# Start addresses of split weights and split activations in on-chip memory, by unused pads and two wider tiles

## The chip, the cores and the metric

One core of one Trainium2 chip runs the whole program. The metric is device microseconds of one execution of the program, as the median of several runs.

## What is computed

Two blocks on 256 tokens of width 1024, batch 1, all in float32. The first block is two layers; the second takes its output as x and is one layer with a small context of 256 tokens and a mixture of 16 experts. Cut to what matters here:

```python
def hybrid_layer(x, mem, pos, g_mix, w_in, w_pa, w_pb, w_pm, w_o, g_mem, w_mkv, g_mlp, w_up, w_down):
    h = rms_norm(x, g_mix)
    z = h @ w_in
    ...
    y = (gates[:, :, 0] * (o_a @ w_pa) + gates[:, :, 1] * (o_b @ w_pb)
         + gates[:, :, 2] * (o_m @ w_pm))
    x = x + y @ w_o
    hm = rms_norm(x, g_mlp)
    x = x + jnp.square(jax.nn.relu(hm @ w_up)) @ w_down
    return x
...
    x = x + g1[:, None, :] * out_l
    h_l = modulate(rmsnorm(x, norm2[l]), sh2, sc2)
    x = x + g2[:, None, :] * ec_moe(h_l, w_router[l], w_e_gate[l], w_e_up[l], w_e_down[l])
```

Behind `out_l` stand a latent attention with 8 heads and a gated recurrent mixer with 4 heads, both fed by projections with `w_in_2`. `ec_moe` lets each expert take 32 tokens and runs gate, up and down products of 1024 by 1024 for each.

## The kernel before, in words

**Split products.** All projections and the two MLPs are computed with split operands. A weight tile of 128 partitions by 2048 floats is loaded into pool `wrp` (tile `wr`, four buffers, `load_w`). `pieces` (L331) cuts it into pieces of 512 columns. ScalarE casts a piece to the format fp32r (the high part, L347), and VectorE, or at times GpSimd, subtracts the high part from the original and writes the rest (the low part, L353 and L351). Activations are split likewise into a high and a low part (`split_x`). `three` (L356) then issues three matmuls for a product: high weights with high activations, high with low, low with high. In `w_stationary` (L366) a block of 128 columns of the weights is loaded into TensorE and 256 columns of activations are streamed; in `x_stationary` (L378) it is the other way round. Every matmul has a weight load of its own, which TensorE issues while the matmul ahead of it runs. All matmuls of the helper `mm` carry line L290.

**Places.** The split pieces live in seven places, used in turn (L321 to L340): four in the tile `wh` of pool `whl`, three in a tile also named `wh` of pool `b1p`. `places.append(places.pop(0))` moves to the next place with every piece:

```python
    whx = whl.tile([128, 2, WH * PIECE], FR, tag="w", name="wh")
    wx_ = b1p.tile([128, 2, WX * PIECE], FR, name="wh")
```

When the second MLP is done, pool `b1p` is closed and the four places of `whl` remain (L1583). A place's high part and low part start at multiples of 2048 bytes from the start of their tile, and a block of 128 columns at multiples of 512, so the start of the tile modulo 128 bytes is the start of every operand in it modulo 128. The same holds for the split activations: `hx` (layer input, and the MLP's), `ux` (MLP hidden), `zq` (attention output), `mx` (memory), `xh` (context), `kvx` and `qx` (latents of the second block).

**Where tiles lie.** Pools are stacked from the low addresses in the order in which they are opened: `cst`, `per`, `sm`, `wrp`, `whl`, and behind them the pools of each stage (`lp0`, `ap0`, `mp0`, `bp`, `x2p` and so on). `b1p`, `ew0`, `yp`, `ew1` and `rt` are stacked from the high end downwards. A tile's size is rounded up to 32 bytes. So a pad moves all tiles stacked behind it.

**Order.** The program is in stages: memory keys; layer 0 (projections, three kinds of attention, gates, output product); its MLP; layer 1; its MLP; then the second block (context path, recurrent mixer, latent attention), up to about 1127 us; the router; and the experts. The order of TensorE is written by hand. In attention-like stages a `Filler` issues a few microseconds of projection matmuls between the links of a softmax chain. Weight loads are issued on SP's queue when a buffer comes free. The experts' weights (tile `ew`) are loaded into 23 slots made of freed tiles and then reused, on the same queue.

`readout` (L1350) scales the recurrent mixer's output; its tile `skip` is a column of 8 floats for each partition. `scg`, also 8 floats, is used once ahead of the second block (L1619). `srow` and `macc` (L567) are the last tiles of `b1p`.

Of the kernel before, what the change touches and what calls it, by code (L numbers as in the profile page):

```python
# [8 lines left out]
FT = mybir.dt.float32  # L9
# [214 lines left out]
def in_turn(*gens):  # L224

    gens = list(gens)
    while gens:
        g = gens.pop(0)
        for c in g:
            yield c  # L230
            if c is None:
                gens.append(g)
                break
# [8 lines left out]
def fused_kernel(ctx: ExitStack, tc: tile.TileContext, I, out):  # L242
# [5 lines left out]
    cst = ctx.enter_context(tc.tile_pool(name="cst", bufs=1))  # L248
    per = ctx.enter_context(tc.tile_pool(name="per", bufs=1))
    sm = ctx.enter_context(tc.tile_pool(name="sm", bufs=4))  # L250
    wrp = ctx.enter_context(tc.tile_pool(name="wrp", bufs=WR, reuse_waits="tile"))
    whl = ctx.enter_context(tc.tile_pool(name="whl", bufs=1, reuse_waits="tile"))
    accp = ctx.enter_context(tc.tile_pool(name="accp", bufs=2, space=PSUM))
    flp = ctx.enter_context(tc.tile_pool(name="flp", bufs=2, space=PSUM))
    wk = ctx.enter_context(tc.tile_pool(name="wk", bufs=2, space=PSUM))
# [17 lines left out]
    b1p = b1.enter_context(tc.tile_pool(name="b1p", bufs=1, side="right"))  # L273
# [8 lines left out]
    def vc(n, j=0, w=1):  # L282
        o = vcols[n][0] + j
        return vbuf[:, o:o + w]
# [4 lines left out]
    def mm(o, l, r, st, sp):  # L289
        PE.matmul(o, l, r, start=st, stop=sp, skip_group_check=True)  # L290
# [6 lines left out]
    def acc_tile(nm):  # L297
        return accp.tile([128, 512], FT, tag="acc", name=nm)

    def fl_tile(nm):  # L300
        return flp.tile([128, 512], FT, tag="fl", name=nm)
# [152 lines left out]
    def rstd_cols(ssum, n, nm, bank=None):  # L454

        ps = (bank or acc_tile)("ps_" + nm)
        halves = [ssum] if len(ssum.shape) == 2 else [ssum[:, i] for i in range(ssum.shape[1])]
        for t in range(2):
            for i, v in enumerate(halves):
                mm(ps[:, t:t + 1], v[:, t * 128:(t + 1) * 128], ones[:, 0:1], t + i == 0, i == len(halves) - 1)  # L460
        r = sm.tile([128, 2], FT, tag="rc_" + nm, name="rc_" + nm, bufs=2)
        with tc.high_priority(offset=HR):
            V.tensor_scalar(r, ps[:, 0:2], 1.0 / n, EPS, op0=OP.mult, op1=OP.add)
            G.tensor_tensor(r, r, mhalf[:, 0:2], op=OP.pow)
        return r

    def bcast_rows(col2, dst, bank=None):

        ps = (bank or acc_tile)("ps_bc")
        for t in range(2):  # L470
            across(ps[:, t * 128:(t + 1) * 128], col2[:, t:t + 1], t == 0)
        with tc.high_priority(offset=HB):
            V.tensor_copy(dst, ps[:, 0:256])

    def updated(dn):

        for j in range(4):
            if dn:
                V.tensor_tensor(xT[:, 2 * j:2 * j + 2], xT[:, 2 * j:2 * j + 2], pair(dn[j]), op=OP.add)
            yield 2 * j  # L480
            yield 2 * j + 1
# [84 lines left out]

    srow = [b1p.tile([128, 1024], FT, name="srow")]  # L567
    macc = b1p.tile([128, 2, 48], FT, name="macc")

    def layer(l, lp, ap, start):  # L570
        xs, ssum = start
# [379 lines left out]
    def pool(st, nm, side="left"):  # L951
        return st.enter_context(tc.tile_pool(name=nm, bufs=1, side=side, reuse_waits="tile"))
# [12 lines left out]
    def modulated(src, rb, sc, sh, tp, emit, eng=None):  # L965

        for k in range(8):
            t = tp.tile([128, 256], FT, tag="modt", name="modt", bufs=2)
            (eng or V).scalar_tensor_tensor(t, src[:, k], sc[:, k:k + 1], rb, op0=OP.mult, op1=OP.mult)
            emit(k, t, sh[:, k:k + 1])  # L970
            yield
# [377 lines left out]

    def readout(hm, ss, xc, tzg, tp):  # L1350

        skip = tp.tile([128, 8], FT, name="skip")
        V.tensor_scalar(skip, vc("mls", 0, 8), 0.5, None, op0=OP.mult)
        V.tensor_scalar(ss, ss, 1.0 / 256, EPS, op0=OP.mult, op1=OP.add)
        G.tensor_tensor(ss, ss, mhalf, op=OP.pow)
        for h in range(4):
            for t in range(2):
                hv = hm[:, t, h * 256:(h + 1) * 256]
                V.tensor_scalar(hv, hv, ss[:, t * 4 + h:t * 4 + h + 1], None, op0=OP.mult)
        F.fill(FRO[0])  # L1360
        for j in range(4):
            F.fill(FRO[1])
            ps = acc_tile("hT")
            for i in range(2):
                for t in range(2):
                    k = 2 * j + i
                    PE.transpose(ps[:, i * 256 + t * 128:i * 256 + t * 128 + 128], hm[:, t, k * 128:(k + 1) * 128],
                                 ident)
            u = tp.tile([128, 2, 256], FT, tag="ro", name="ro", bufs=2)
            for i in range(2):  # L1370
                k = 2 * j + i
                A.activation(u[:, i], xc[:, k], AF.Copy, scale=skip[:, k:k + 1])
                V.scalar_tensor_tensor(u[:, i], ps[:, i * 256:(i + 1) * 256], vc("mln", k), u[:, i], op0=OP.mult,
                                       op1=OP.add)
            sl = slice(2 * j, 2 * j + 2)
            V.scalar_tensor_tensor(u, tzg[0][:, sl], 1.0, u, op0=OP.add, op1=OP.mult)
            V.scalar_tensor_tensor(hm[:, :, j * 256:(j + 1) * 256], tzg[1][:, sl], 1.0, u, op0=OP.add, op1=OP.mult)
# [220 lines left out]
    with ExitStack() as es:  # L1598
        fp = pool(es, "b2c")
        xcc = fp.tile([128, 8, 256], FT, name="xcc")  # L1600

        def ctx_path():
            yield from in_turn(ml_features(cx, xcc, kTc, vex[0], gp, wg, fp),
                               keys_values(0, cx, kn[0], vt[0], kp0, fp))

        share[0] = SH1[0]
        cg = F.add(ctx_path())

        s1 = fp.tile([128, 256], FT, name="s1")
        s2 = fp.tile([128, 256], FT, name="s2")  # L1610
        for k in updated(dn):
            for s_, sc, eng in ((s1, 1.0, G), (s2, vc("g_fin", k), V)):
                d = s_ if k == 0 else fp.tile([128, 256], FT, tag="sqf", name="sq", bufs=3)
                A.activation(d, xT[:, k], AF.Square, scale=sc)
                if k:
                    eng.tensor_tensor(s_, s_, d, op=OP.add)
            F.fill(FX[2])
        share[0] = SH1[1]
        scg = fp.tile([128, 8], FT, name="scg")  # L1619
        V.tensor_tensor(scg, sc1[:, 0], vc("g_fin", 0, 8), op=OP.mult)  # L1620
        F.fill(FX[0])
        r1 = rstd_cols(s1, 1024, "fin")
        ps = acc_tile("ps_s2")
        for t in range(2):
            mm(ps[:, t:t + 1], s2[:, t * 128:(t + 1) * 128], ones[:, 0:1], t == 0, True)
        r2 = fp.tile([128, 2], FT, name="r2")
        V.scalar_tensor_tensor(r2, ps[:, 0:2], 1.0 / 1024, r1, op0=OP.mult, op1=OP.mult)
        V.tensor_tensor(r2, r2, r1, op=OP.mult)
        V.tensor_scalar(r2, r2, EPS, None, op0=OP.add)
        G.tensor_tensor(r2, r2, mhalf[:, 0:2], op=OP.pow)  # L1630
        V.tensor_tensor(r2, r2, r1, op=OP.mult)
        F.fill(FX[1])
        rb2 = fp.tile([128, 256], FT, name="rb2")
        bcast_rows(r2, rb2)
        rb1 = fp.tile([128, 256], FT, name="rb1")
        bcast_rows(r1, rb1)
        for _ in modulated(xT, rb2, scg, modT[:, 0, 0:8], fp, into(hh, hl)):
            F.fill(FX[3])
        share[0] = SH1[2]
        F.need(cg)  # L1640

        sh2 = modT[:, 0, 24:32]
        ss = per.tile([128, 8], FT, name="ssh")
        lb0 = per.tile([128, 16], FT, name="lb0")
        lb_ps = fl_tile("lb0")
        sw = fp.tile([128, 8, 16], FT, name="sw")
        V.tensor_tensor(sw, vc("wrt", 0, 128).rearrange("p (k e) -> p k e", k=8),
                        sh2[:, :, None].to_broadcast([128, 8, 16]), op=OP.mult)
        sws = fp.tile([128, 16], FT, name="sws")
        V.tensor_reduce(sws, sw.rearrange("p k e -> p e k"), axis=AX.X, op=OP.add)  # L1650
        mm(lb_ps[:, 0:16], ones, sws, True, True)
        V.tensor_copy(lb0, lb_ps[:, 0:16])
        for k in range(8):
            A.activation(xT[:, k], xT[:, k], AF.Copy, scale=vc("g_fin", k))
            G.tensor_tensor(xT[:, k], xT[:, k], rb1, op=OP.mult)
# [48 lines left out]
    with ExitStack() as es:  # L1704
        tp = pool(es, "b2k")
# [324 lines left out]
```

## Time and profile before

| what | value |
|---|---|
| median of three runs | 1569.76 us (1569.51 to 1571.85) |
| the profiled execution | 1572.26 us |
| its span in the trace | 1570.5 us |
| granted TensorE clock, mean over the span | 0.945 |
| TensorE matmuls, weight loads | 1372.3 us (87%), 1138.6 us (72%) |
| VectorE, ScalarE, GpSimd | 914.0, 666.6, 242.3 us |
| transfers | 404.87 MB, mean 258 GB/s |

Times of single instructions come from the profiled execution. PE is TensorE's matmul stream, PEld its weight loads, DVE is VectorE, ACT ScalarE, POOL GpSimd, SP the queue that issues the transfers. A matmul lasts longer than the distance to the next one, since they are pipelined; the distance (the step) is what counts in a dense stream, and a window cut at the start of a run and at the start of the next gives it. A clock of 1.00 is the full granted clock.

### The profile page before, as it was taken

The numbers are of one execution on the slowest core, as the hardware profiler recorded it, in microseconds if no ns is written. First come the engines' busy times: TensorE is split into PE (matmuls) and PEld (weight loads), VectorE is DVE, ScalarE is ACT, GpSimd is POOL, SyncE is SP. The second block draws the span as 40 slices with busy tenths as digits, with TensorE's granted clock in tenths as the row PEclk, the third lists the DMA queues.
The fourth block names the chain that finished last, engine by engine and source line by source line (L and its number), as shares of the span: only waits on it lengthen the run. The fifth ranks groups of instructions, "written<-read, shape, count | busy, mean of one in ns | idle before, by whom it ended". The sixth has DMA issues, their size and how long they took to land. (4 is left out here: it accounts for less than half of the span.)

```text
span 1570.5 us, 27054 instructions
## 1 busy us (share of the span) xinstructions
PE 1372.3 (87%) x10903; PEld 1138.6 (72%) x10903; DVE 914.0 (58%) x1615; ACT 666.6 (42%) x1341; POOL 242.3 (15%) x204
## 2 busy tenths in 40 slices
PE   7999999999999999999998999999798656555555
PEld 7999989999999999999996899989642111111114
DVE  8976788777787589899887875975410000000001
ACT  7566555555557556555565666554320000000001
POOL 3100022222210016433252211210100000000000
PEclk9999999999999999999999999999999777877878
DMA  8544437666543456768853322465889999999997
GB/s 319 201 139 158 162 131 285 242 238 218 187 162 135 148 202 237 281 250 304 293 186 124 134 82 81 142 242 187 348 324 426 427 429 427 428 427 427 429 426 325
DMA packets 50557, 404.87 MB, mean 258 GB/s; under 512 B 5504, under 2 KB 7424, under 8 KB 14464
## 3 DMA queue, kind: packets, MB, share of 16 engines
q1 hardware_dynamic: 50288, 403.04, 66.5%
q8 instruction: 85, 1.39, 0.3%
q14 instruction: 40, 0.33, 0.1%
q10 hardware_dynamic: 144, 0.11, 0.0%
HBM read 402.08 MB, written 1.05 MB: 257 GB/s over the span
## 5 line engine op out<-in xcount | busy, mean ns | idle before, releaser
L347 ACT CAST wh<-wr 128x512 fp32r<-128x512 f32 (+1 forms) x647 | 388.3, 615 | 295.5 <-PE up L290 55.7
L353 DVE TENSOR_TENSOR wh<-wr,wh 128x512 fp32r<-128x512 f32 (+1 forms) x563 | 418.4, 756 | 128.6 <-ACT wh L347 124.7
L290 PE MATMUL up<-hx,wh 128*128 128x256 f32 x1536 | 190.9, 282 | 4.9 <-DVE hx L428 2.2
L290 PEld LDWEIGHTS up<-hx,wh 128*128 128x128 f32 x1536 | 184.8, 189 | 7.5 <-DVE hx L428 3.3
L351 POOL TENSOR_TENSOR wh<-wr,wh 128x512 fp32r<-128x512 f32 (+1 forms) x84 | 122.3, 1457 | 438.0 <-ACT wh L347 369.5
L290 PE MATMUL dn<-ux,wh 128*128 128x256 f32 x1536 | 186.7, 281 | 0.3 <-POOL wh L351 0.3
L290 PEld LDWEIGHTS dn<-ux,wh 128*128 128x128 f32 x1536 | 183.9, 189 | 0.5 <-POOL wh L351 0.5
L1948 DVE TENSOR_TENSOR ew<-up,ew 128x512 f32<-128x512 f32 x8 | 5.5, 691 | 249.5 <-PE up L290 249.5
L290 PE MATMUL gate<-hx,wh 128*128 128x256 f32 x1152 | 138.8, 281 | 0.0
L290 PEld LDWEIGHTS gate<-hx,wh 128*128 128x128 f32 x1152 | 136.3, 190 | 1.4 <-issue 1.4
L290 PE MATMUL y<-ew 128*32 128x128 f32 (+1 forms) x896 | 77.3, 494 | 43.2 <-DMA ew<-in_w_e_down_dram 42.6
L290 PE MATMUL up<-ew,xsr 128*32 128x512 f32 x384 | 64.2, 802 | 52.7 <-DMA ew<-in_w_e_up_dram 52.7
L290 PE MATMUL gate<-ew,xsr 128*32 128x512 f32 x384 | 63.4, 792 | 46.9 <-DMA ew<-in_w_e_gate_dram 46.9
L1942 ACT ACTIVATE ew<-gate 128x512 f32<-128x512 f32 x8 | 4.8, 597 | 209.9 <-PE gate L290 208.6
L290 PEld LDWEIGHTS y<-ew 128*32 128x32 f32 x896 | 28.2, 122 | 90.0 <-DMA ew<-in_w_e_down_dram 50.8
L290 PEld LDWEIGHTS up<-ew,xsr 128*32 128x32 f32 x384 | 12.1, 128 | 105.8 <-DMA ew<-in_w_e_up_dram 75.8
L290 PEld LDWEIGHTS gate<-ew,xsr 128*32 128x32 f32 x384 | 12.1, 127 | 95.7 <-DMA ew<-in_w_e_gate_dram 63.7
L290 PE MATMUL tanh<-hx,wh 128*128 128x256 f32 x576 | 77.0, 287 | 0.2 <-DVE wh L353 0.2
L290 PE MATMUL z<-hx,wh 128*128 128x256 f32 x576 | 72.5, 284 | 4.1 <-ACT wh L347 1.2
L290 PEld LDWEIGHTS z<-hx,wh 128*128 128x128 f32 x576 | 69.1, 190 | 6.6 <-DVE hx L428 1.6
L290 PEld LDWEIGHTS tanh<-hx,wh 128*128 128x128 f32 x576 | 71.5, 191 | 1.2 <-DVE wh L353 0.5
L925 DVE SCALAR_TENSOR_TENSOR wr<-wr,srow 128x1024 f32<-128x1024 f32 x48 | 67.0, 1404 | 0.1
(451 smaller groups left out, 1985.6 us busy)
## 6 DMA issues: line engine op xcount, KB each, us to landing
ew<-in_w_e_up_dram SPq DMA_DIRECT2D x26, 2048.0 KB, 22.1
ew<-in_w_e_down_dram SPq DMA_DIRECT2D x25, 2048.0 KB, 21.4
ew<-in_w_e_gate_dram SPq DMA_DIRECT2D x24, 2048.0 KB, 21.2
wr<-in_w_up_dram SPq DMA_DIRECT2D x32, 1024.0 KB, 4.8
wr<-in_w_down_dram SPq DMA_DIRECT2D x32, 1024.0 KB, 5.0
wr<-in_w_gates_dram SPq DMA_DIRECT2D x24, 1024.0 KB, 4.8
wr<-in_w_modT_dram SPq DMA_DIRECT2D x24, 1024.0 KB, 4.9
wr<-in_w_in_dram SPq DMA_DIRECT2D x24, 1024.0 KB, 4.8
```

The lines of the kernel that those rows point to most:

```text
L290: PE.matmul(o, l, r, start=st, stop=sp, skip_group_check=True)
L347: A.copy(hv, src)
L351: behind[1] = G.tensor_tensor(lv, src, hv.bitcast(FT), op=OP.subtract).ins
L353: behind[0] = V.tensor_tensor(lv, src, hv.bitcast(FT), op=OP.subtract).ins
L925: V.scalar_tensor_tensor(d, w[:, j], 0.5, srow[v], op0=OP.mult, op1=OP.mult, accum_out=macc[:, v, 2 * i + j:2 * i + j + 1])
L1942: A.activation(h[:, j * 512:(j + 1) * 512], gate[j], AF.Silu)
L1948: V.tensor_tensor(h[:, c], up[j], h[:, c], op=OP.mult)
```

## The change

It adds three tiles that nothing writes or reads (32 bytes ahead of `wrp`, 64 bytes behind `whl`, 32 bytes as the last tile of `b1p`) and makes `skip` and `scg` 128 bytes wide instead of 32, of which the same first 8 floats are used.

```diff
+    pad1 = ctx.enter_context(tc.tile_pool(name="pad1", bufs=1))
+    pad1.tile([128, 8], FT, name="pad1")
     wrp = ctx.enter_context(tc.tile_pool(name="wrp", bufs=WR, reuse_waits="tile"))
     whl = ctx.enter_context(tc.tile_pool(name="whl", bufs=1, reuse_waits="tile"))
+    pad2 = ctx.enter_context(tc.tile_pool(name="pad2", bufs=1))
+    pad2.tile([128, 16], FT, name="pad2")
...
     macc = b1p.tile([128, 2, 48], FT, name="macc")
+    b1p.tile([128, 8], FT, name="pad3")
...
-        skip = tp.tile([128, 8], FT, name="skip")
+        skip = tp.tile([128, 32], FT, name="skip")[:, 0:8]
...
-        scg = fp.tile([128, 8], FT, name="scg")
+        scg = fp.tile([128, 32], FT, name="scg")[:, 0:8]
```

In the built programs the instructions of every engine, their order and what they wait for are the same before and after, but for line numbers. What differs is where tiles start. In bytes modulo 128:

| tile (pool) | before | after |
|---|---|---|
| split weights `wh`, four places (`whl`) | 32 | 64 |
| split weights `wh`, three places (`b1p`) | 96 | 64 |
| split activations `hx`, `ux`, `zq`, `mx`, `xh` | 32 | 0 |
| split activations `kvx`, `qx` | 64 | 0 |
| keys of the memory (`kmh`, `kml`), read with `qm` | 96, with 32 | 64, with 0 |
| loaded weights `wr`, and expert slots in `wrp` and `whl` | 32 | 64 |
| other tiles of the stages' pools on the low side, `ew` in them | 32 (behind `scg`, `skip`: 96, 64) | 0 (32, 0) |
| `ew` in `ew0`, `yp`, `ew1`; `rt`, `xT`, constants | 96; 0 to 96 | the same |

## Rows read from the trace of the kernel before

**Rows 1.** Page, parts 1 and 2: busy us of the engines; GB/s in 40 slices.

```profile
PE 1372.3 (87%) x10903; PEld 1138.6 (72%) x10903; DVE 914.0 (58%) x1615; ACT 666.6 (42%) x1341; POOL 242.3 (15%) x204
...
GB/s 319 201 139 158 162 131 285 242 238 218 187 162 135 148 202 237 281 250 304 293 186 124 134 82 81 142 242 187 348 324 426 427 429 427 428 427 427 429 426 325
```

**Rows 2.** Windows by stage: busy us (instructions) of PE, PEld, DVE, ACT, POOL; clock, DMA.

```profile
160.00:200.00 40.00, 40.00 (x344) 40.00 (x343) 29.65 (x45) 21.96 (x36) 2.90 (x2) 1.00 0.53 181
240.00:400.00 160.00, 160.00 (x1345) 160.00 (x1345) 126.83 (x188) 86.36 (x148) 33.55 (x23) 1.00 0.67 243
520.00:600.00 80.00, 80.00 (x685) 80.00 (x684) 58.05 (x87) 42.18 (x70) 7.81 (x6) 1.00 0.56 191
600.00:640.00 40.00, 37.63 (x311) 36.80 (x310) 38.77 (x52) 25.61 (x55) 25.89 (x23) 1.00 0.67 255
680.00:720.00 40.00, 39.45 (x331) 38.78 (x330) 38.19 (x60) 21.15 (x40) 14.01 (x10) 1.00 0.73 269
1127.00:1570.00 443.00, 280.41 (x2110) 87.22 (x2108) 33.31 (x73) 25.31 (x55) 2.41 (x3) 0.82 0.97 407
```

**Rows 3.** Chain that ended last, pieces in order of time: start, us, what.

```profile
1053.85 2.87 PE tanh L290 x24
1056.72 3.46 PE pvl L290 x16
...
1138.58 425.70 issue
```

**Rows 4.** Waits of TensorE: us in total, times, longest.

```profile
PE up L290 <- DMA ew<-in_w_e_up_dram: 52.7, 24, 3.0
```

**Rows 5.** Windows of TensorE alone: stretch, us, busy (matmuls), clock, DMA share, GB/s.

```profile
530.90:534.98 4.08, 4.08 (x39) 1.00 0.34 102
534.98:540.74 5.76, 5.76 (x51) 1.00 0.55 206
339.90:345.66 5.76, 5.76 (x50) 1.00 0.35 127
345.66:349.91 4.25, 4.25 (x39) 1.00 0.60 200
1017.22:1021.43 4.21, 4.21 (x37) 1.00 0.87 317
```

**Rows 6.** Tile wh: duration ns min/median/max of the instructions that write it.

```profile
L347 ACT CAST wh<-wr x647: 387/620/659, 4.4 to 1117.0; 128x512 fp32r<-128x512 f32 x158, 128x256 fp32r<-128x256 f32 x4
L353 DVE TENSOR_TENSOR wh<-wr,wh x563: 407/685/1792, 4.8 to 1117.9; 128x512 fp32r<-128x512 f32 x186, 128x256 fp32r<-128x256 f32 x2
```

**Rows 7.** Windows of TensorE's matmuls on tile wh alone (columns of rows 5).

```profile
0.00:224.10 224.10, 194.12 (x1585) 1.00 0.54 193
224.10:409.00 184.90, 181.48 (x1504) 1.00 0.64 234
409.00:789.30 380.30, 355.85 (x2962) 1.00 0.61 219
789.30:1127.00 337.70, 216.20 (x1623) 0.98 0.44 162
```

**Rows 8.** The same for tile kvx, then for tile qx, up to 1127 us.

```profile
0.00:1127.00 1127.00, 27.26 (x144) 0.99 0.55 199
...
0.00:1127.00 1127.00, 14.14 (x108) 0.99 0.55 199
```

**Rows 9.** Windows of matmuls on wh in stretches where TensorE also waits (as rows 7).

```profile
0.00:40.00 40.00, 29.78 (x219) 1.00 0.83 313
800.00:840.00 40.00, 32.88 (x237) 0.96 0.44 155
840.00:880.00 40.00, 22.83 (x171) 0.91 0.30 108
880.00:920.00 40.00, 20.61 (x166) 0.96 0.22 80
1000.00:1040.00 40.00, 31.48 (x222) 1.00 0.63 233
```

## The prediction

> **What bounds the kernel now.** I read the page first. TensorE is busy 87% of the span; VectorE 58%, ScalarE 42% [rows 1]. The last quarter of the GB/s line is flat at about 427, so the kernel has two halves, which the windows by stage show. [...] From 1127 on the transfers of the expert weights are busy 97% of the time [rows 2]. The chain of waits says the same: matmul after matmul up to 1127 us, then 425.70 us with nothing on the chain that an engine could shorten [rows 3], while TensorE waits for expert weights [rows 4]. So a faster matmul before 1127 us brings the end forward, because the first expert products, which free the slots for the next loads, begin earlier; a faster one behind it brings nothing.
>
> The view that matters is the windows of TensorE alone, cut at the edges of the weight places. A piece of split weights is 512 columns: four blocks of 128, three matmuls each, twelve in all, each with a weight load of its own. Four places lie in pool whl (32 modulo 128) and three in b1p (96), used in turn; so runs of 48 and of 36 matmuls alternate, with activations at 32 throughout. At 530.90 us a run of 36 takes 4.08 us, **113.3 ns** a matmul; the run of 48 behind it takes 5.76 us, **120.0 ns** [rows 5]. (The counts shown are a little higher, since matmuls in flight at an edge count too.) Shape, work and clock are the same; only the bytes differ at which weights start. In the first MLP, 48 take 5.76 us again, 120.0 ns, and 36 take 4.25 us, 118.1 ns. With activations at 64 and weights at 32 (tile qx), 36 take 4.21 us, 116.9 ns [rows 5]. Behind 800 us b1p is closed and all weights are at 32: 24 matmuls take 2.87 us, 119.6 ns [rows 3]. So the step of a matmul depends on the start bytes of its two operands.
>
> [...]
>
> **What the change does, part by part.** The pads, the wider skip and the wider scg issue no instruction, and order and waits stay as they are; only addresses move. Weights go to 64 and activations to 0, so every pair lies 64 apart. No row shows 64 and 0. The nearest row is weights 96, activations 32, also 64 apart, at 113.3 ns. I take that, and keep as ends of the unknown step 120.0 ns (the worst row) and 108.1 ns: sixteen fp32 passes of 256 columns take 3.46 us, 216.2 ns each [rows 3], at half the column rate of these matmuls, and half of that is what a matmul would take that lost nothing to its neighbour.
>
> ScalarE's and VectorE's parts of the split write places at 32 and 96 alike, and their medians are 620 and 685 ns with ScalarE between 387 and 659 [rows 6]: no second price shows, so moving these costs nothing I can see. Transfers ran at 426 to 429 GB/s to slots at 32 and at 96 [rows 1]; I put 0 on the new starts, with 2 us either way (2 of 427 on 426 us).
>
> The sum, by counts on tile wh: 1585 + 1504 + 2962 = 6051 matmuls up to 789 us, of which 4/7, 3458, read whl and 3/7, 2593, read b1p; 1623 behind [rows 7], of which 144 belong to kvx (48 of 512 columns among them, which I leave out) and 108 to qx [rows 8], and 1 is counted twice at the edge, so 1370 are plain.
> - whl: 3458 + 1370 = 4828, from 120.0 to 113.3, 6.67 ns each: 32.2 us.
> - b1p in the first MLP: 3/7 of 1504 = 645, from 118.1: 3.1 us. The other 1948: nothing.
> - kvx and qx at 256 columns: 96 + 108 = 204, from 116.9: 0.7 us.
>
> Together 36.0 us. Not all of it lies on the path. In five stretches of 40 us TensorE also waits, and its matmuls on wh fill time between links of a chain on VectorE and ScalarE: 219 + 237 + 171 + 166 + 222 = 1015 [rows 9]. There a shorter fill turns into a longer wait, and I count half: 1015 x 6.67 / 2 = 3.4 us lost. VectorE does not become the bound at this step: at 680 to 720 us it works 38.19 of 40, at 600 to 640 us 38.77 [rows 2], and these stretches shrink by 4/7 of 331 and of 311 matmuls x 6.67 ns, 1.3 and 1.2 us. That is just its slack, so what is late next there is VectorE's part of the split.
>
> That leaves 32.6 us. The profiled execution took 1572.26 us, 2.5 above the median of the runs: 1572.26 - 32.6 - 2.5 = **1537 us**.
>
> **The rivals.**
> - *No loss at all.* What still parts 113.3 ns from half an fp32 pass hangs on starts at 32 and 96 as well, and goes with them; the step falls to 108.1 ns. For it: the fp32 passes lose nothing at 32 [rows 3]. Against: no row of these matmuls is below 113.3, and qx, at 64, has 116.9. Then 4828 x 11.9 + 1948 x 5.2 + 645 x 10.0 + 204 x 8.8 = 57.5 + 10.1 + 6.5 + 1.8 = 75.9 us, less 1015 x 11.9 / 2 = 6.0, less 3 at 600 to 640 and 680 to 720 us, where 642 matmuls x 9.0 ns = 5.8 us meet a slack of VectorE of 3.0: 66.9 us, 1503. [...]
> - *Only the distance counts, with both levels.* Blocks 64 apart run at 113.3 in most stages and at 118.1 in the first MLP. If a quarter of all pairs falls on the slow level, as now (645 of 2593), the mean is 114.5: 4828 x 5.5 + 204 x 2.4 = 27.0, less 2.8, is 24.2 us: 1546.
> - *The slow level everywhere.* At 118.1: 4828 x 1.9 = 9.2 won, 1948 x 4.8 = 9.4 and 204 x 1.2 = 0.2 lost: 1570.
> - *Slower.* What counts is the 96 itself. The pair 64 and 0 then behaves like 32 and 32, 120.0 ns for all, and b1p loses its lead: 1948 x 6.67 + 645 x 1.9 + 204 x 3.1 = 14.8 us where TensorE is full: 1585. It decides from the mean step of today up: (4828 x 120.0 + 1948 x 113.3 + 645 x 118.1 + 204 x 116.9) / 7625 = 118.0 ns. Against it: of the five windows only same start bytes give 120.0 [rows 5].
> - *Nothing*, the stages being bound by VectorE's split after all: 1570. Against it: TensorE's own busy time is the whole stage [rows 2].
>
> **How the numbers follow.** Chances: 0.42 for the forecast, 0.25 for no loss at all, 0.21 for both levels, 0.04 for the slow level, 0.05 for slower, 0.03 for nothing. What a measurement here can tell from no change is 0.2%, 3.1 us. Faster is the first three, 0.88; same the fourth and the last, 0.07; slower 0.05. The range reaches from 1508, which leaves out the end of the no-loss case, to 1560, which takes in both levels with up to two thirds on the slow one; the last three cases lie outside.
>
> **What would show it right or wrong.** Windows of TensorE: runs of 48 and 36 no longer differ, and 24 matmuls behind 800 us take 2.72 us (113.3) rather than 2.87; 2.59 would be the no-loss case, 2.83 the slow level. The pieces of the chain before 1127 us move up by some 32 us, and the 425.70 us behind stay within 2. VectorE's share at 600 to 720 us rises; a wait of TensorE for the split of weights there would be the first loss. Wrong would be steps as now, or steps of 113.3 with an end that stays: then a chain on VectorE and not TensorE sets the stages.

## The result and the profile after

The changed kernel takes **1552.01 us** (median of 4 runs, 1551.37 to 1552.58) against 1570.25 us (4 runs) before: a ratio of 0.9882, 95% interval 0.9865 to 0.9899, 18.2 us less. The forecast was 1537 us in a range of 1508 to 1560; the chance went 0.88 to faster. So the sign and the range held, and 18.2 of 32.6 forecast us came. The profiled execution took 1552.58 us, span 1550.8.

The page, busy us of the engines and the GB/s line (answers to [rows 1]):

```profile
PE 1353.3 (87%) x10903; PEld 1117.5 (72%) x10903; DVE 913.0 (59%) x1615; ACT 662.4 (43%) x1341; POOL 241.9 (16%) x204
...
GB/s 323 201 142 156 169 141 280 259 251 233 161 185 133 155 204 253 284 254 312 318 164 109 109 82 89 205 203 195 321 382 427 427 430 427 429 428 429 427 429 316
```

TensorE is busy 19.0 us less for the same 10903 matmuls, the weight loads 21.1 us less; VectorE, ScalarE and GpSimd are within 1%, and the flat quarter is where it was, at 427. The chain that ended last (answers to [rows 3]) shows the same: its last piece is as long as before, 425.62 against 425.70 us, and starts at 1118.95 instead of 1138.58, 19.6 us earlier.

```profile
1060.84 2.83 PE tanh L295 x24
...
1081.52 8.48 PE wo L295 x72
...
1118.95 425.62 issue
```

24 matmuls of the filler take 2.83 us, 117.9 ns each, where the prediction asked for 2.72 and named 2.83 as the slow level. The windows of TensorE alone say where it came out as forecast and where not (columns as in [rows 5]: stretch, us, busy (matmuls), clock, DMA share, GB/s). The first two are a run of 36 from b1p and one of 48 from whl in layer 1's projections, the last three 48, 36 and 48 in the MLP of layer 1:

```profile
518.27:522.36 4.08, 4.08 (x38) 1.00 0.45 122
522.36:527.80 5.44, 5.44 (x50) 1.00 0.55 200
693.95:699.60 5.65, 5.65 (x50) 1.00 0.77 304
699.60:703.68 4.08, 4.08 (x38) 1.00 0.95 323
703.68:709.12 5.44, 5.44 (x50) 1.00 0.92 345
```

4.08/36 and 5.44/48 are 113.3 ns, the level of the forecast, now for both pools. But 5.65/48 is 117.7 ns, and that run has the same four places, the same start bytes modulo 256 and the same clock as the next run of whl, of 5.44 us. **One pair of start bytes has two levels**, and a stream mostly keeps the one on which it is: of the 537 steps from one matmul's start to the next that stood between 160 and 224 us before the change, all are now at 113.3. The windows of matmuls on wh by stage (answers to [rows 7]):

```profile
0.00:220.50 220.50, 192.15 (x1585) 1.00 0.55 196
220.50:397.80 177.30, 173.73 (x1505) 1.00 0.67 244
397.80:771.30 373.50, 347.47 (x2959) 1.00 0.62 222
771.30:1107.60 336.30, 213.19 (x1625) 0.98 0.44 164
```

Busy time on wh falls by 2.0, 7.8, 8.4 and 3.0 us, 21.1 in all. A finer count takes the distance from each plain matmul's start to the next one's, for the 7360 of 256 columns ahead of the router whose next one follows within 140 ns in both traces: the mean goes from 118.2 to 114.9 ns, 24.2 us. 65% of them are near 113.3 and 35% on the upper level. Some 4.5 us of the 24.2 are lost in waits, and 19.6 arrive.

### The profile page after: what moved, and what is told of

It is laid out like the page before. It is cut to its first block, busy times and chain, and to the rows that moved or that the text cites. A ratio compares the mean times of both kernels' runs of the same rounds, so it can differ in the third digit from the quotient of the medians.

```text
span 1550.8 us, 27054 instructions
## 1 busy us (share of the span) xinstructions
PE 1353.3 (87%) x10903; PEld 1117.5 (72%) x10903; DVE 913.0 (59%) x1615; ACT 662.4 (43%) x1341; POOL 241.9 (16%) x204
## 5 line engine op out<-in xcount | busy, mean ns | idle before, releaser
L295 PE MATMUL up<-hx,wh 128*128 128x256 f32 x1536 | 185.5, 278 | 6.2 <-DVE wh L358 2.7
L295 PEld LDWEIGHTS up<-hx,wh 128*128 128x128 f32 x1536 | 179.1, 188 | 9.2 <-DVE wh L358 4.1
L295 PE MATMUL dn<-ux,wh 128*128 128x256 f32 x1536 | 180.0, 277 | 0.4 <-POOL wh L356 0.4
L295 PEld LDWEIGHTS dn<-ux,wh 128*128 128x128 f32 x1536 | 177.1, 188 | 0.8 <-POOL wh L356 0.6
L295 PE MATMUL gate<-hx,wh 128*128 128x256 f32 x1152 | 135.5, 278 | 0.0
L295 PEld LDWEIGHTS gate<-hx,wh 128*128 128x128 f32 x1152 | 133.1, 188 | 1.4 <-issue 1.4
L1925 DVE SCALAR_TENSOR_TENSOR ew<-y,gsl,xT 128x512 f32<-128x512 f32 (+2 forms) x10 | 6.4, 644 | 107.1 <-PE y L295 107.0
## 6 DMA issues: line engine op xcount, KB each, us to landing
ew<-in_w_e_down_dram SPq DMA_DIRECT2D x25, 2048.0 KB, 21.1
```

The source lines that it names most:

```text
L1925: V.scalar_tensor_tensor(dst[:, c0:c0 + w], src, gsl[:, G4:G4 + 1], rows[:, 0, c0:c0 + w], op0=OP.mult, op1=OP.mult)
```

## The experiments

From here on a kernel is told by its distance: the start of the weights minus that of the activations, modulo 256 bytes, as in `w_stationary`, which has most matmuls. Before, it is 0 in whl (160 and 160) and 192 in b1p (96 and 160); in the changed kernel 192 in whl (192 and 0) and 64 in b1p (64 and 0). Modulo 128, as the prediction counted, 64 and 192 are one. Theory A in the expectations says that they are not, theory B that they are, theory C that the starts and not the distance count. Ratios are to the kernel before, with the 95% interval behind them. Shares of steps on a level are counts over the steps of one trace, the upper level being all above 115.5 ns.

**All weights 64 behind, the rest alike.**

```diff
-    pad2.tile([128, 16], FT, name="pad2")
+    pad2.tile([128, 48], FT, name="pad2")
...
-    b1p.tile([128, 8], FT, name="pad3")
+    b1p.tile([128, 40], FT, name="pad3")
...
-        skip = tp.tile([128, 32], FT, name="skip")[:, 0:8]
+        skip = tp.tile([128, 64], FT, name="skip")[:, 0:8]
...
-        scg = fp.tile([128, 32], FT, name="scg")[:, 0:8]
+        scg = fp.tile([128, 64], FT, name="scg")[:, 0:8]
```

> Edit, against the changed kernel: split activations go from 0 to 128 modulo 256, the places in b1p from 64 to 192 and kvx and qx with the activations; the places of whl stay at 192. So both sets of weights start 64 bytes behind the activations modulo 256 (today whl 192 and b1p 64). Theory A (the two start bytes count modulo 256: weights 64 behind the activations draw a stream from 117.8 to 113.3 ns, weights 192 behind leave it at the level on which it began): nearly all plain matmuls run at 113.3; the trace of the changed kernel holds 11.6 us above that level up to 1108 us, of which 0.6 to 0.8 comes back, so 1543 us (1541 to 1547), ratio to the kernel before 0.983. Theory B (only modulo 128 counts, so 64 and 192 are one case, and the level is an accident of each stretch): as the changed kernel, 1552 us (1549 to 1555). Theory C (weights at 64 and activations at 0 are what counts, not their distance): the same distance with both 64 higher loses some of the gain, over 1555 us.

1549.42 us (4 runs, 1549.08 to 1551.49), ratio 0.988 (0.9866 to 0.9895). The time misses A's 1541 to 1547 and lies within B's; it can't be told from the changed kernel's. The mean step is 114.5 ns, 25% on the upper level instead of 35%: a move in A's direction, but a quarter of the steps stay up at a distance that should have drawn all of them down.

**All weights 192 behind**: as the last, but `pad2` stays at 16 floats, so activations stay at 0.

> Edit, against the changed kernel: only the places in b1p go from 64 to 192 modulo 256 (kvx and qx from 128 to 0); activations stay at 0 and whl at 192, so all weights start 192 bytes behind the activations. Modulo 128 every start is as in the changed kernel. Theory A: nothing draws a stream down any more, most plain matmuls behind a break stay at 117.8 ns; 7360 of them x (117.8 - 114.9) = 21 us, of which 0.6 to 0.8 reach the end: 1567 us (1560 to 1570), the gain gone. Theory B and theory C: no change, 1552 us (1549 to 1555).

1563.29 us, ratio 0.9968 (0.9948 to 0.9988), within A's range. Its ten runs scatter from 1556.36 to 1568.83, where the two sets of four runs of the changed kernel scatter by 1.2 and 2.5 us. The mean step is 116.6 ns with 72% on the upper level. Modulo 128 nothing moved, so B and C fall. Windows of TensorE alone, 36 matmuls in the first MLP, then 48 in the second:

```profile
302.84:306.92 4.08, 4.08 (x38) 1.00 0.90 317
619.13:624.78 5.65, 5.65 (x50) 1.00 0.53 190
```

113.3 and 117.8 ns, each held through most of its stretch: 88% of the steps of the first MLP are on the lower level and less than 1% of those of the second. So 192 has both levels too, but is more often on the upper one; and which one a long stretch gets, would explain the scatter (only one execution has a trace, so that is argued and not shown).

**128 and 0 behind**: `pad2` 32 floats, or none.

> Edit, against the kernel with 64 behind: activations at 64 modulo 256 with all weights at 192, 128 behind. Theory A names no level for 128: anything from 113.3 to 120 ns, 1543 to 1585 us. Theory B: 128 is 0 modulo 128, so 120.0 ns everywhere: 7360 x (120.0 - 114.9) = 37.5 us, of which 0.6 to 0.8 reach the end, 1578 us (1574 to 1585).

> Edit, against the kernel with 64 behind: activations at 192 modulo 256 like all weights, 0 apart, all starts multiples of 64. Theories A and B: 120.0 ns everywhere as in the kernel before for its pairs of 32 and 32, 1578 us (1574 to 1585), slower than the kernel before by some 0.5%. Theory C (a start at a multiple of 64 is what gains): faster than the kernel before, 1540 to 1560 us.

128 behind: 1576.48 us, ratio 1.0052 (1.0037 to 1.0067), mean step 119.0. 0 behind: 1581.8 us, ratio 1.0082 (1.0067 to 1.0097), mean step 119.9. Windows of 48 matmuls in layer 1's projections, of 128 and then of 0:

```profile
549.47:555.16 5.69, 5.69 (x50) 1.00 0.46 150
```

```profile
541.40:547.16 5.76, 5.76 (x50) 1.00 0.49 186
```

118.6 and 120.0 ns. That multiples of 64 alone would gain, as C has it for the last run, is out: with 0 behind all starts are multiples of 64, and the kernel is the slowest of all. These four kernels differ in one pad alone, and their medians lie up to 32 us apart.

**The distances by themselves.**

> A kernel of its own, which leaves all of the computation out but the copy of a part of x: streams of 72 matmuls of 256 columns in the same format and order of operands (high with high, high with low, low with high), for activations at 0, 32, 64 and 128 modulo 256 and weights 0 to 224 bytes behind in steps of 32, for some finer distances, for 320 and 448, each behind a break; then the eight distances again directly behind a stream that runs with 64 and behind one with 0. Theory A: 64 ends at 113.3 ns wherever the activations start, 0 at 120.0, 192 at 117.8 behind a break and behind the stream of 0, and at 113.3 behind the stream of 64; 320 and 448 as 64 and 192. Theory B: 64 and 192 alike, 0 and 128 alike, 32 and 160 alike. Theory C: the level changes with the start of the activations at one distance. For 32, 96, 128, 160 and 224 no theory but B names a level beyond 113.3 to 120; any value under 113.3 would be a better choice for the kernel.

Windows of TensorE alone in the middle of seven streams, 48 matmuls each: activations at 0 with 0, 64, 160, 192, 224; then at 64 with 64; then at 128 with 192.

```profile
30.22:35.98 5.76, 5.76 (x50) 1.00 0.00 0
49.12:54.56 5.44, 5.44 (x50) 1.00 0.00 0
77.25:83.01 5.76, 5.76 (x50) 1.00 0.00 0
86.77:92.42 5.65, 5.65 (x50) 1.00 0.02 3
96.13:101.73 5.60, 5.60 (x50) 1.00 0.00 0
199.85:205.50 5.65, 5.65 (x50) 1.00 0.01 3
312.54:317.98 5.44, 5.44 (x50) 1.00 0.00 0
```

0 and 160 are at 120.0 ns, 224 at 116.7, 32 at about 118.3; 64 and 192 are at 113.3 or 117.8, and hold it for 72 matmuls. (96 and 128 come to several means between 117.3 and 120.1, by stream.) No other engine computes here and almost nothing is transferred, so neither the levels nor their holding come from traffic. Behind a stream on 113.3, 192 had no trial (the one ahead of it happened to be on 117.8, and it stayed there); behind one of 0 it came to 113.3. So A's rule that 192 only keeps what it finds is wrong: the level is set where the stream begins.

**Starts of 32 modulo 64, and 224 behind.** Against the kernel before: pads of 192 bytes behind whl and in b1p, skip and scg 64 floats wide; then the pad behind whl 32 bytes.

```diff
     whl = ctx.enter_context(tc.tile_pool(name="whl", bufs=1, reuse_waits="tile"))
+    pad2 = ctx.enter_context(tc.tile_pool(name="pad2", bufs=1))
+    pad2.tile([128, 48], FT, name="pad2")
...
+    b1p.tile([128, 48], FT, name="pad3")
```

> Edit, against the kernel before: only a pad of 192 bytes behind whl, one of 192 in b1p, and skip and scg 256 bytes wide. Weights stay at 160 modulo 256 in whl and come to 160 in b1p, activations come to 96: all weights 64 behind, at starts that are 32 modulo 64. If only the distance counts: as the kernel with all weights 64 behind at starts 192 and 128, ratio to the kernel before 0.988 (1547 to 1553 us), with about a quarter of the plain matmuls on the level of 117.8. If starts at multiples of 64 are needed (theory C): ratio over 0.993.

> Edit, against the run before it: the pad behind whl 32 bytes in place of 192, so activations come to 192 and all weights to 224 behind modulo 256. The map of single streams has 116.7 ns for 224, behind every break alike; qx and kvx of the kernel before stand 224 behind as well, at 116.8 to 117.2. If the map carries over: 116.7 in all stages, also where 64 behind was at 117.8, so against the changed kernel's mean of 114.9 7360 x 1.8 = 13 us more, of which 0.7 to 0.9 reach the end: 1562 us (1559 to 1566). If the level comes from other engines' traffic and not from the distance: two levels again, with shares as at 64 or 192, 1549 to 1566.

Weights at 160 and activations at 96, 64 behind: 1557.71 us, ratio 0.9933 (0.9907 to 0.9958), 52% on the upper level. The same distance at 192 and 128 has 0.988 and 25%, so the start counts beside the distance after all. 224 behind: 1565.06 us, ratio 0.997 (0.9958 to 0.9983), at 5.60 us for 48 matmuls, 116.7 ns, as in the map, and that in every stage (means of 116.7 to 117.2):

```profile
540.59:546.19 5.60, 5.60 (x50) 1.00 0.46 146
```

The map carries over to the kernel; so [rows 5] had a third case in qx, which stands 224 behind, at 116.9.

**Entries.**

> A kernel of its own, which leaves all of the computation out but the copy of a part of x: streams of 36 matmuls for weights 0 to 252 bytes behind activations that start at 0, in steps of 4; then, for 64, 192, 8 and 224 behind, 29 entries each, in which a break and one matmul of 32 to 256 columns stand ahead of a stream of 24. If the level is drawn at the entry: 64 and 192 show 113.3 in some entries and 117.8 in others, 64 more often 113.3 than 192, and 224 always 116.7, 8 always 115.5. If 64 and 192 differ only by chance, their shares are alike. A distance whose steps are all below 113.3, or always at it, would be a better choice.

> A kernel of its own as the second map (all of the computation left out but the copy of a part of x): 29 entries each, a break and one matmul of 32 to 256 columns ahead of a stream of 24, for distances that came to 113.4 ns by themselves there (52, 76, 88, 180, 204 with activations at 0, 76 also at 128 and 96, 180 at 160), for 64 with activations at 32, 96 and 128, and 192 at 128. If 76 and 180 draw every stream to 113.4, nearly all of their entries end there, against 17 of 29 for 64 at 0 and 1 of 29 for 192. If they were lucky draws, their shares lie between those two. If the absolute start counts beside the distance, the shares of 64 differ between starts; the kernel with 64 behind at starts of 32 modulo 64 had 52% of its plain steps on the slow level, that at multiples of 64 25%, so a lower share at 32 and 96 than at 128 would name the start as the reason.

The last 12 steps of each stream of 24, counted as on 113.3 when their mean is under 114.5:

| activations at | weights behind | entries on 113.3 | the others |
|---|---|---|---|
| 0 | 64 | 17 of 29 | 117.7 |
| 32 | 64 | 12 of 29 | 117.8 |
| 96 | 64 | 14 of 29 | 117.8 |
| 128 | 64 | 27 of 29 | 117.7 |
| 0 | 192 | 1 of 29 | 117.7 |
| 128 | 192 | 6 of 29 | 117.7 |
| 0, 96, 128 | 76 | 22, 29, 23 of 29 | 120.0 |
| 0 | 52, 88 | 27, 24 of 29 | 117.8, 116.7 |
| 0, 160 | 180 | 19, 8 of 29 | 117.8 to 118.4 |
| 0 | 204 | none | 120.0 to 123.3 |
| 0 | 8 | none | 115.4 to 115.7 |
| 0 | 224 | none | 116.7 (21), 117.8 (8) |

Two entries at 32 with 64 behind, which differ in the matmul ahead of them (32 and 40 columns):

```profile
582.48:583.84 1.36, 1.36 (x14) 1.00 0.00 0
586.26:587.68 1.41, 1.41 (x14) 1.00 0.00 0
```

12 matmuls in 1.36 and 1.41 us. So the level is drawn at the entry, and distance and start set the odds. Neither 180 nor 224 behaved as expected: 180 did not draw every stream down, and 224 is not always at 116.7. And 204, at 113.3 in its one stream of the second map, came to it in none of 29 entries here: that one was a lucky draw. The kernel with 64 behind has its activations at 128, the best of these starts, the one with 52% above at 96. Of the 64 distances in steps of 4 bytes, no stream of the second map settled below 113.2 ns.

**The best pair of the map in the kernel: 76 behind 96.** Against the kernel before; the pads (160 bytes) and the wider skip and scg are left out of what is shown.

```diff
+    def shifted(pl, n, **kw):
+        t = pl.tile([128, 2 * n + 8], FR, name="wh", **kw)[:, 3:2 * n + 3]
+        return t.rearrange("p (h n) -> p h n", h=2)
+
-    whx = whl.tile([128, 2, WH * PIECE], FR, tag="w", name="wh")
-    wx_ = b1p.tile([128, 2, WX * PIECE], FR, name="wh")
+    whx = shifted(whl, WH * PIECE, tag="w")
+    wx_ = shifted(b1p, WX * PIECE)
```

> Edit, against the kernel with all weights 64 behind at starts of 32 modulo 64: the tiles of the places are 32 bytes longer and read from their fourth float on, so weights start 76 behind the activations at 96 modulo 256, the pair that ended at 113.4 ns in 29 of 29 entries in the third map; the pads behind whl and in b1p are 32 bytes shorter, so nothing but the memory's keys moves otherwise. If the entry shares of the map carry over: almost no plain step of weights against columns of activations on a slow level, 1 to 3 us above 113.33 where the changed kernel has 11.6, 0.6 to 0.8 of the difference at the end: 1545 us (1543 to 1548), ratio to the kernel before 0.985. If in the kernel something else draws the level (breaks of another kind, traffic of other engines): a mean step of 114.5 to 116, 1549 to 1560 us. If starts at 12 modulo 32 cost ScalarE or VectorE time at the split, their medians of 620 and 685 ns rise and the gain is less.

> The changed kernel once more, for a comparison on one chip: 1552 us (1550 to 1554) by its first runs, and the same share of slow steps within a few per cent if the entries repeat from execution to execution.

1549.83 us, ratio 0.9878 (0.9861 to 0.9896), beside the changed kernel's 1551.81, ratio 0.9887 (0.987 to 0.9905), on the same chip. That is above the 1543 to 1548 of the map's shares. The mean step is 114.25 ns with 17% above, 29.0 us won against 24.2; the split is as quick as before (medians 619 and 687 ns). In the dense stages the map carried over, with 98 to 100% of the steps on the lower level; in the attention stages it did not (65% in layer 0's, 48% in layer 1's, 67% behind the second MLP). And 5.9 us instead of 4.5 go to waits, and 23.2 arrive. It and the kernel with 64 behind (ratio 0.988) are 2 to 3 us ahead of the changed one by their medians, less than the 0.2% that a measurement here can tell. The changed kernel's second trace has the same mean, 114.9, and the same 35%.

**Without the pad in b1p.**

```diff
-    b1p.tile([128, 8], FT, name="pad3")
```

> Edit, against the changed kernel: the last pad, that in b1p, is left out, so the three places of b1p stay at 96 as before the change while everything else moves (whl 192 behind the activations, b1p 96). The maps have 117.2 to 120.0 ns for 96 behind, by entry. If they carry over: 2593 plain matmuls up to 789 us go from about 114 to 118.6, 12 us of which most lies where TensorE is full, and runs of whl lose the draw to 113.3 that the runs of b1p gave them, up to 8 us more: 1565 us (1560 to 1572), most of the gain gone. If the pad in b1p is worth only what the forecast gave the b1p term (3.1 us): 1555 us.

1560.19 us, ratio 0.9943 (0.9926 to 0.9959): 8.4 us over the 1551.81 of the changed kernel's second runs, nearly half of what the change won, since without it b1p goes to 96 behind: the mean step of b1p is 117.8 ns here and 114.3 in the changed kernel. Windows of 48 matmuls of whl and of 36 of b1p, 113.4 and 117.4 ns:

```profile
548.21:553.65 5.44, 5.44 (x50) 1.00 0.43 151
543.98:548.21 4.22, 4.22 (x38) 1.00 0.57 233
```

The second half of that expectation failed: up to 789 us whl, 192 behind, has 69% of its steps on the lower level here and 76% in the changed kernel, and so does not need runs at 64 between its own. But where all places are 192 behind, it has 34%, and between 160 and 224 us (as the kernel before has them) none, where it has nearly all with 64 or 96 in between. That a change of distance inside a stream brings a new draw would explain it; no run tests it by itself.

## Why the prediction was right, and where it was too large

**What bounds the kernel: right.** Up to 1127 us TensorE was busy for 1091.9 us before the change, and what it won and kept up to the router moved the end by as much: the chain's last piece starts 19.6 us earlier and kept its length [rows 3], and the span is 19.7 us shorter.

**The step of 113.3 for all: the term that was mis-sized.** "No row shows 64 and 0 ... I take that" took [rows 5] at 530 us for the level of a pair 64 apart. That level exists, and it is the lower of two: the mean over all is 114.9. By the terms of the sum, each matmul put to the place that it reads: whl won 21.5 of 32.2 us (18.3 of 23.1 up to 789 us, 3.2 of 9.1 behind), b1p 2.6 of 3.1, kvx and qx 0.1 of 0.7.

The row with 118.1 in the same group was the other level, and the first MLP, where b1p stood on it throughout, was no special case: in the trace of the kernel before, 42% of b1p's steps are on the upper level, and 23% outside the first MLP. So "the other 1948: nothing" came out (-0.3 us) because b1p drew about as often badly after the change as before, and not because it stood at 113.3. The range held by reaching over the rival with both levels, and not by the step that was forecast. By stage, the forecast of the step terms by [rows 7] and [rows 8] against the count of steps:

| stage (us, before) | forecast | won | mean step after |
|---|---|---|---|
| 0 to 224 | 6.0 | 4.1 | 115.6 to 160 us, 113.3 behind |
| 224 to 409, first MLP | 8.8 | 8.3 | 113.5 |
| 409 to 789 | 11.3 | 8.4 | 115.8 to 520 us, 113.4 to 590, 114.5 behind |
| 789 to 1127 | 9.9 | 3.3 | 117.2 |
| sum | 36.0 | 24.2 | 114.9 |

In the first MLP, long and unbroken, the forecast holds to half a microsecond in nine; between 590 and 789 us, where the second MLP is as dense, 26% of the steps are on the upper level. Where the order puts short fillings between the links of a chain, each begins anew and, as the maps suggest, draws anew; and behind 789 us only whl is left, at 192 behind, the distance with the poor odds (117.2 ns there; with all weights 64 behind the same stage has 115.6). The rival with both levels had the two levels right and put a quarter of all pairs on the upper one; 35% were. It gave 1546, the nearest of the cases.

**The waits: right in kind.** 3.4 us were taken off, 4.5 were lost: 1.4 behind 789 us, where 3.3 were won on steps, close to the half that was assumed, 1.6 between 590 and 789, the other 1.5 ahead of that. VectorE's slack in the second MLP was taken as just enough. Windows of the kernel before (busy us of PE, PEld, DVE, ACT, POOL; clock, DMA share, GB/s), then the same two pieces of work after the change, then in the kernel with 76 behind:

```profile
660.00:680.00 20.00, 20.00 (x174) 20.00 (x173) 18.87 (x28) 9.42 (x18) 7.06 (x4) 1.00 0.66 238
680.00:700.00 20.00, 19.45 (x160) 18.79 (x159) 19.78 (x36) 10.32 (x20) 5.54 (x3) 1.00 0.57 207
```

```profile
643.50:663.40 19.90, 19.90 (x173) 19.90 (x172) 18.77 (x29) 10.02 (x20) 6.21 (x5) 1.00 0.70 259
663.40:684.60 21.20, 19.42 (x159) 18.54 (x158) 20.99 (x37) 10.33 (x20) 6.68 (x4) 1.00 0.60 212
```

```profile
662.40:684.10 21.70, 19.17 (x159) 18.27 (x158) 21.48 (x37) 10.33 (x20) 7.12 (x4) 1.00 0.60 209
```

VectorE is busy 20.99 of 21.20 us: the piece got 1.2 us longer, and what TensorE had won up to there was partly handed back. In the kernel with 76 behind TensorE comes a microsecond earlier, VectorE is full again at 21.48 of 21.70, and the piece ends 0.5 us earlier. The new wait is TensorE's for VectorE's part of the split, as the prediction named it (us in total, times, longest, in the second piece; before, then after):

```profile
PE up L290 <- DVE wh L353: 0.2, 1, 0.2
PE up L295 <- DVE wh L358: 1.4, 2, 1.1
```

A window of 40 us had hidden that the slack of 1.8 us lay outside these 20.

**What was costed at nothing** stayed so: the split's medians are 620 and 686 ns against 620 and 685 [rows 6], and the last piece of the chain is 0.1 us shorter.

```profile
L352 ACT CAST wh<-wr x647: 388/620/666, 4.3 to 1097.5; 128x512 fp32r<-128x512 f32 x158, 128x256 fp32r<-128x256 f32 x4
L358 DVE TENSOR_TENSOR wh<-wr,wh x563: 407/686/1796, 4.8 to 1098.4; 128x512 fp32r<-128x512 f32 x186, 128x256 fp32r<-128x256 f32 x2
```

**The other rivals.** No loss at all fell: no stream of the maps settled below 113.2 ns, and no stage of a kernel has a mean step below 113.3. Its 108.1 ns was the author's estimate, half of the 216.2 ns of an fp32 pass [rows 3]. Those passes take 216 ns at other starts too (16 in 3.45 us after the change, in 3.46 in the kernel with 0 behind), but 216.2 is 1.91 times the lower level of these matmuls, 113.3, and no run shows the half for them. The slow level everywhere fell: 65% of the steps are on the lower one. Slower as told (the pair 64 and 0 at 120.0) fell too, but its step is real at 0 and 160 behind: the kernel with 0 behind is 0.8% slower than before. Nothing, for VectorE's split, fell with the 19.6 us.

## What to carry to other kernels

Where each matmul loads its own weights, look at the distance from start to start in a dense stream, sorted by the start bytes of both operands, modulo 256 at least (all weights 64 and all weights 192 behind, alike modulo 128, took 1549.4 and 1563.3 us here), before counting on shape alone; one pad was worth 2% between the best and the worst distance (1549.4 and 1581.8 us, at 64 and 0 behind). A level read from one stretch is one draw: take the mean over all stages, and expect the worse one where streams are short and begin behind a break (117.2 ns behind 789 us here, 113.5 in the unbroken first MLP). And look for the engine with the least slack in windows as short as the piece of work, for it takes the gain back there.

## What had not been expected of the hardware

Two steady levels, 113.3 and 117.8 ns, for one pair of start bytes, held for hundreds of matmuls (537 steps at 113.3 with all weights 64 behind, 597 at 117.8 with all weights 192 behind, in one dense stretch each) and set at the entry (12 to 27 of 29 entries on the lower one at 64 behind, depending on where the activations start). The step depends on start bytes down to 4. Windows of 12 matmuls in three streams of the second map, at 72, 76 and 80 behind, are at 118.3, 113.4 and 118.8 ns; at 8 behind every entry settled at 115.5, at 76 behind the entries were at 113.3 or 120.0.

```profile
123.40:124.82 1.42, 1.42 (x14) 1.00 0.00 0
128.54:129.91 1.36, 1.36 (x14) 1.00 0.04 12
133.59:135.02 1.43, 1.43 (x14) 1.00 0.00 0
```

What it is in an entry that decides, was not found.
